# Linear attention with ReLU features: loads of two octets at a time, and one uniform loop in place of a loop with a hand-written end

## The chip, the cores and the metric

The kernel runs on one core of a Trainium2 chip. The metric is the device time of one execution in microseconds (us), as the median of several runs; lower is better. Durations of single instructions come from one profiled execution of the same kernel.

## The reference

```python
# Q, K, V: (8, 12, 512, 64) float32, 96 heads of 512 rows
Q_feat = np.maximum(0, Q)
K_feat = np.maximum(0, K)
KV = np.einsum('bhkd,bhkv->bhdv', K_feat, V)          # 64 x 64 per head
K_sum = np.sum(K_feat, axis=2)
numerator = np.einsum('bhqd,bhdv->bhqv', Q_feat, KV)
denominator = np.einsum('bhqd,bhd->bhq', Q_feat, K_sum)
out = numerator / (denominator[:, :, :, None] + 1e-10)
```

## The kernel before

The 96 heads are worked in 12 octets of eight heads (`NO` = 12), and an octet's K and V in two groups of four heads (`NG` = 24; octet `o` has the groups `2o` and `2o+1`). An octet's K, V and Q are 1 MB each in float32. All loads but those of octet 0's K and V go through POOL's DMA queue and are cast to bf16 on the way, so that a profile that counts the bytes written shows half of them. An octet's result is stored as 1 MB of float32.

The work of one octet `o`, by its functions:

- `prep(g)`: VectorE (DVE) makes the ReLU of K of group `g`, masked in two ways (`kf`, two instructions), and the first masked copy of V (`vo`, one). `prep_v(g, eng)` makes the second masked copy of V, on ScalarE (ACT) or on DVE. Both copies are needed by the matmuls of that group.
- `mm_kv(g)`: 16 matmuls on TensorE (PE) that sum K^T V of a group into its half of the PSUM tile `ps_kv`.
- `evac_kv(o, gs, share)`: four copies from `ps_kv` to the block-diagonal weights `kvd`, on ACT (with `share`, two of the four on DVE).
- `transp`, `relu_q`, `qt(o)`: 16 PE transposes of an octet's Q in two halves, and the ReLU of each half on ACT, which gives `qt`.
- `denom(o)`: 16 small matmuls for the denominators, then on DVE a masked add (`own`), a reduction (`den`) and a reciprocal (`rec`).
- `out_t(o)`: eight matmuls in two halves of four, each half copied from PSUM to `ot_sb` by ACT.
- `back(o, j)`: eight PE transposes (float32) of half `j` of `ot_sb` into PSUM; `norm(o, j, ...)`: DVE multiplies that half by `rec` into `o_sb`. `backs(o)` does both halves and then calls `store(o)`.
- `idle(n, o)`: `n` matmuls whose result nobody reads, in the last octets.

Instructions of one engine run in the order in which the program writes them; engines wait for one another through semaphores. PSUM has two buffers for the outputs of `out_t` and `back` together (`pou`), and two for the transposes of Q (`pqt`).

In SBUF there is a ring of `RING` = 6 octets for K, V and Q. At the start the loads of octets 1 to 6 are queued, two octets a transfer (`FIRST`): K, V, Q of octets 1 and 2, then of 3 and 4, then of 5 and 6. Each `store(o)` for `o` from 1 to 5 is followed on POOL's queue by the loads of octet `o + 6`: in three transfers for octets 7 and 8, in five (K and V by groups) for octets 9 to 11 (`PAIRS` = 9). The last two octets are stored from SP's queue, octet 11 in two halves.

For octets 0 to 8 (`SAME` = 8) one iteration of the loop is: `mm_kv` of both groups, `evac_kv(o)`, `prep` and `prep_v` (on ACT) of the next octet's first group, `backs(o - 1)`, `denom(o)`, `out_t(o)`, `prep` and `prep_v` (on DVE) of the next octet's second group, `qt(o + 1)`. From octet 8 on the order changes: `mm_kv` and `evac_kv` of the next octet stand ahead of `qt(o + 1)`, and `backs(o)` follows in the same iteration. The last two octets are written out one step after another, with `evac_kv` by groups and part of ACT's work given to DVE.

Of the kernel before, what the change touches and what calls it, by code (L numbers as in the profile page):

```python
# [10 lines left out]
def kernel(  # L11
# [7 lines left out]
    nc = tc.nc  # L19
    B, H, S, D = Q.shape  # L20
    assert D == 64
    P = 128
    D1 = D + 1
# [4 lines left out]
    RQ = S * 8 // P  # L28
    NHG = 4
    U = RQ // 2  # L30
    NG = NH // NHG
    NO = NG // 2
# [3 lines left out]
    fp32 = mybir.dt.float32  # L36
    bf16 = mybir.dt.bfloat16
    Act = mybir.ActivationFunctionType
# [50 lines left out]

    q_sb, k_sb, v_sb = {}, {}, {}  # L90

    PAIRS = NO - 3
    RING = DELAY + 1
    FIRST = (2, 2, 2)
    k_all = consts.tile([P, 2 * RING, R, D], bf16, name="k_all")
    v_all = consts.tile([P, 2 * RING, R, D], bf16, name="v_all")
    q_all = consts.tile([P, RING + 1, U, 2 * D], bf16, name="q_all")
# [6 lines left out]

    def load_kv(X, tile_, first, n):
        to = 2 * ((first // 2 - 1) % RING) + first % 2
        if n == 1:
            nc.gpsimd.dma_start(out=tile_[:, to].rearrange("p r d -> p (r d)"), in_=X[first], single_packet=True)  # L108
            return
        nc.gpsimd.dma_start(out=tile_[:, to:to + n].rearrange("p n r d -> p n (r d)"),  # L110
                            in_=X[first:first + n].rearrange("n p f -> p n f"), single_packet=True)

# [13 lines left out]
    load_q(0)  # L126
    make_identity(nc, ident)

    def load_octet(o, n=1):
        m = 1 if o >= PAIRS else 2 * n  # L130
        for g in range(2 * o, 2 * (o + n), m):
            load_kv(Kr, k_all, g, m)
            load_kv(Vr, v_all, g, m)
        load_q(o, n)

    o = 1
    for n in FIRST:
        load_octet(o, n)
        o += n
    assert o == RING + 1  # L140

    def zero_masks():
        for h in range(NHG):
# [48 lines left out]
    def prep(g):  # L192
        kf[g] = kfp.tile([P, R, 2, D], bf16, name="kf")
        for s in range(2):
            nc.vector.tensor_scalar(kf[g][:, :, s, :], k_sb[g], scalar1=0.0,  # L195
                                    scalar2=mask[:, 0, s:s + 1], op0=Alu.max, op1=Alu.mult)
        nc.vector.tensor_scalar(vo[g % NB][:, :, 0, 2:D + 2], v_sb[g], scalar1=mask[:, 1, 0:1],  # L197
                                scalar2=None, op0=Alu.mult)

    def prep_v(g, eng):  # L200
        if eng is nc.scalar:
            nc.scalar.activation(vo[g % NB][:, :, 1, 2:D + 2], v_sb[g], Act.Copy, scale=mask[:, 1, 1:2])  # L202
        else:
            nc.vector.tensor_scalar(vo[g % NB][:, :, 1, 2:D + 2], v_sb[g], scalar1=mask[:, 1, 1:2],  # L204
                                    scalar2=None, op0=Alu.mult)

    def mm_kv(g):
        for r in range(R):
            nc.tensor.matmul(  # L209
                ps_kv[:, g % 2, 0:2 * (D + 2)].rearrange("p (t d) -> p t d", t=2),  # L210
                kf[g][:, r, :, :].rearrange("p s d -> p (s d)"), vo[g % NB][:, r, :, 1:D4 - 1],
                start=(r == 0), stop=(r == R - 1), skip_group_check=True)


    def evac_kv(o, gs, share=False):
        for s in range(2):
            for c in range(2):
                copy = nc.vector.tensor_copy if share and c == 1 else nc.scalar.copy
                copy(  # L219
                    kvd[o % NK][64 * c:64 * c + 64, 4 * gs.start + s:4 * gs.stop:2,  # L220
                               c * D1:c * D1 + D1].rearrange(
                        "p (g t) d -> p g t d", t=2),
                    ps_kv[64 * s:64 * s + 64, gs, 0:2 * (D + 2)].rearrange(
                        "p g (t d) -> p g t d", t=2)[:, :, :, c:c + D1])


    def transp(o, i):
        ps = pqt.tile([P, U // 2, P], bf16, name="ps_qt")
        for u in range(U // 2):
            nc.tensor.transpose(ps[:, u, :], q_sb[o][:, i * (U // 2) + u, :], ident)  # L230
        return ps

    def relu_q(o, i, ps, eng=None):
        to = qt_sb[o % NZ][:, i * (U // 2):(i + 1) * (U // 2)]
        if eng is nc.vector:
            nc.vector.tensor_scalar(to, ps, scalar1=0.0, scalar2=None, op0=Alu.max)
        else:
            nc.scalar.activation(to, ps, Act.Relu)  # L238

    def qt(o):  # L240
        for i in range(2):
            relu_q(o, i, transp(o, i))


    def idle(n, o):
        for i in range(n):
# [2 lines left out]

    def out_t(o, halves=range(2)):
        if halves[0] == 0:
            ot[o] = otp.tile([P, U, 8, 16], fp32, name="ot_sb")
        q = qt_sb[o % NZ].rearrange("p u (h c) -> p u h c", h=8)
        for j in halves:
            ps = pou.tile([P, 4, U, 16], fp32, name="ps_ot", tag="ps_out")
            for i in range(4):
                h = 4 * j + i
                nc.tensor.matmul(ps[:, i], kvd[o % NK][:, h, 1:2 * D + 1], q[:, :, h, :],  # L260
                                 start=True, stop=True, skip_group_check=True)
            nc.scalar.copy(ot[o][:, :, 4 * j:4 * j + 4], ps.rearrange("p h u c -> p u h c"))  # L262
# [3 lines left out]
    def denom(o):  # L266
        ps = ps_den[:, 0].rearrange("p (u h c) -> p u h c", u=U, h=8)
        for u in range(U):
            nc.tensor.matmul(ps[:, u], qt_sb[o % NZ][:, u, :], kvd[o % NK][:, :, 0:2 * D1:2 * D1 - 1],  # L269
                             start=True, stop=True, skip_group_check=True)  # L270
        own = rcp.tile([P, U, 8, 2], fp32, name="own")
        nc.vector.scalar_tensor_tensor(
            own.rearrange("p u h c -> p u (h c)"), ps.rearrange("p u h c -> p u (h c)"), 1e-10,
            mask_h.rearrange("p h c -> p (h c)").unsqueeze(1).to_broadcast([P, U, 16]),
            op0=Alu.add, op1=Alu.mult)
        den = rcp.tile([P, RQ], fp32, name="den")
        nc.vector.tensor_reduce(out=den.rearrange("p (u c) -> p u c", c=2),  # L277
                                in_=own.rearrange("p u h c -> p u c h"), op=Alu.add,
                                axis=mybir.AxisListType.X)
        rec[o] = rcp.tile([P, RQ], fp32, name="rec")  # L280
        nc.vector.reciprocal(rec[o], den)
# [9 lines left out]
    def norm(o, j, ps, o_sb):  # L291
        rs = slice(16 * j, 16 * j + 16)
        nc.vector.tensor_tensor(o_sb[:, rs], ps,  # L293
                                rec[o][:, rs].unsqueeze(2).to_broadcast([P, 16, D]), op=Alu.mult)
# [3 lines left out]

    def store(o, o_sb):
        Ov = Or[o].rearrange("p (r d) -> p r d", d=D)  # L300
        if o == NO - 1:
            for j in range(2):
                rs = slice(RQ // 2 * j, RQ // 2 * (j + 1))
                nc.sync.dma_start(out=Ov[:, rs], in_=o_sb[:, rs])
            return
        if o >= NO - 2:
            nc.sync.dma_start(out=Ov, in_=o_sb)
            return
        nc.gpsimd.dma_start(out=Ov, in_=o_sb, single_packet=True)  # L309
        if 0 < o < NO - RING:  # L310
            load_octet(o + RING)

    def out_tile():
        return outp.tile([P, RQ, D], fp32, name="o_sb", tag="o_sb")

    both = slice(0, 2)
    zero8()
    nc.vector.tensor_copy(ident32, ident)
    nc.vector.tensor_reduce(out=mask8k, in_=ident32.rearrange("p (t s b) -> p s t b", t=4, s=2),
# [12 lines left out]
    def backs(o):  # L332
        o_sb = out_tile()
        for j in range(2):
            norm(o, j, back(o, j), o_sb)
        store(o, o_sb)

    def kvs(o):
        mm_kv(2 * o)
        mm_kv(2 * o + 1)  # L340
        evac_kv(o, both)

    SAME = NO - 4
    for o in range(NO - 2):
        if 0 < o <= SAME:
            kvs(o)
        prep(2 * o + 2)
        prep_v(2 * o + 2, nc.scalar)  # L350
        if 0 < o <= SAME:
            backs(o - 1)
        denom(o)
        out_t(o)
        prep(2 * o + 3)
        prep_v(2 * o + 3, nc.vector)
        if o >= SAME:
            kvs(o + 1)
        qt(o + 1)
        if o >= SAME:  # L360
            backs(o)

    o = NO - 2
    g = 2 * NO - 2
    prep(g)
    prep_v(g, nc.vector)
    denom(o)
    out_t(o)
    mm_kv(g)
    evac_kv(o + 1, slice(0, 1))  # L370
    prep(g + 1)
    prep_v(g + 1, nc.vector)

    o_sb = out_tile()
    norm(o, 0, back(o, 0), o_sb)
    ps = back(o, 1)
    mm_kv(g + 1)
    evac_kv(o + 1, slice(1, 2), share=True)
    for i in range(2):
        relu_q(o + 1, i, transp(o + 1, i), nc.vector if i == 1 else None)  # L380
    norm(o, 1, ps, o_sb)
    store(o, o_sb)
    idle(5, o + 1)
    out_t(o + 1, (0,))
    denom(o + 1)
    out_t(o + 1, (1,))
    idle(6, o + 1)
    backs(o + 1)
# [1 line left out]
_INS = ['Q', 'K', 'V']  # L390
_OUTS = [((8, 12, 512, 64), 'float32')]
# [25 lines left out]
```

## Time and profile before

| | |
|---|---|
| median of 3 runs | 126.01 us (125.93 to 126.33) |
| the profiled execution | 126.86 us, of which the span from the first to the last instruction is 125.1 us |
| busy, share of the span | PE 86.3 us (69%), DVE 83.2 us (67%), ACT 80.6 us (64%), POOL 26.5 us (21%) |
| mean granted PE clock | 0.931 |
| HBM | 37.75 MB read, 12.58 MB written: 402 GB/s over the span |

How to read the views: the page cuts the span into 40 equal slices, and a digit is the busy share of a slice in tenths (9 is 90% or more); `PEclk` is the granted PE clock in the same way, `DMA` the mean busy share of the 16 DMA engines. The chain that ended last is followed back from the last instruction, at each step to what released it; in order of time its lines read: start, duration, what. A timeline row reads: start, duration, engine, line, operation, tiles, shapes, number of instructions merged, and in brackets the idle time of the engine before it and who ended it. A row of windows gives a stretch's busy time and number of instructions on each engine, the granted PE clock, the share of DMA and GB/s. `L209` is line 209 of the kernel; busy matmuls are pipelined and their ends are modelled.

### The profile page before, as it was taken

The numbers are of one execution on the slowest core, as the hardware profiler recorded it, in microseconds if no ns is written. First come the engines' busy times: TensorE is split into PE (matmuls) and PEld (weight loads), VectorE is DVE, ScalarE is ACT, GpSimd is POOL, SyncE is SP. The second block draws the span as 40 slices with busy tenths as digits, with TensorE's granted clock in tenths as the row PEclk, the third lists the DMA queues.
The fourth block names the chain that finished last, engine by engine and source line by source line (L and its number), as shares of the span: only waits on it lengthen the run. The fifth ranks groups of instructions, "written<-read, shape, count | busy, mean of one in ns | idle before, by whom it ended". The sixth has DMA issues, their size and how long they took to land.

```text
span 125.1 us, 2615 instructions
## 1 busy us (share of the span) xinstructions
PE 86.3 (69%) x1067; PEld 77.6 (62%) x1067; DVE 83.2 (67%) x192; ACT 80.6 (64%) x112; POOL 26.5 (21%) x47
## 2 busy tenths in 40 slices
PE   0005884089898998959989897799596496888500
PEld 0005563089787897839978786698494494876400
DVE  2719716920997979797297984967909819977700
ACT  0009966544989989896598988658669466646000
POOL 6942020000100901203311122144333321000000
PEclk9999999558999999995999999859999999999995
DMA  4999999999999999999999999999999999999991
GB/s 84 389 321 206 212 210 217 214 210 210 215 219 208 212 212 218 214 321 419 217 204 307 282 218 264 324 212 238 347 214 226 356 224 216 349 422 424 430 390 76
DMA packets 9836, 32.67 MB, mean 261 GB/s; under 512 B 736, under 2 KB 736, under 8 KB 8160
## 3 DMA queue, kind: packets, MB, share of 16 engines
q0 software_dynamic: 9104, 28.31, 94.5%
q1 hardware_dynamic: 576, 3.15, 6.6%
q10 hardware_dynamic: 144, 1.05, 2.2%
q8 instruction: 8, 0.13, 0.4%
q14 instruction: 4, 0.03, 0.1%
HBM read 37.75 MB, written 12.58 MB: 402 GB/s over the span
## 4 chain that ended last, share of the span: by engine, by line
DMA 44%; DVE 23%; PE 19%; POOL 4%; ACT 2%; issue 2%; DVEq 1%; POOLq 0%
DMA q_all<-in_Q_dram 28%; DMA v_all<-in_V_dram 16%; DVE o_sb L293 13%; PE ps_kv L209 8%; PE ps_bk L287 6%; PE ps_qt L230 3%; DVE kf L195 3%; ACT ot_sb L262 2%; DVE vo_all L197 2%; PE ps_ot L260 1%; DVE vo_all L204 1%; POOL k_all L110 1%; POOL v_all L110 1%; DVE den L277 1%; DVEq L412 1%
## 5 line engine op out<-in xcount | busy, mean ns | idle before, releaser
L293 DVE TENSOR_TENSOR o_sb<-ps_bk,rec 128x1024 f32<-128x1024 f32 x24 | 28.3, 1218 | 20.0 <-PE ps_bk L287 20.0
L209 PE MATMUL ps_kv<-vo_all,kf 128*128 128x132 bf16 x352 | 26.9, 238 | 4.9 <-DVE vo_all L204 4.4
L209 PEld LDWEIGHTS <-kf 128*128 128x128 bf16 x352 | 24.8, 106 | 6.2 <-issue 3.5
L230 PE MATMUL ps_qt<-ident,q_all 128*128 128x128 bf16 x192 | 15.5, 245 | 15.9 <-DMA q_all<-in_Q_dram 15.8
L262 ACT COPY ot_sb<-ps_ot 128x1024 f32<-128x1024 f32 x24 | 24.0, 1013 | 3.8 <-PE ps_ot L260 2.9
L219 ACT CAST kvd<-ps_kv 64x260 bf16<-64x260 f32 (+1 forms) x46 | 16.5, 359 | 15.1 <-PE ps_kv L209 13.9
L238 ACT ACTIVATE qt<-ps_qt 128x1024 bf16<-128x1024 bf16 x23 | 22.4, 1025 | 3.6 <-PE ps_qt L230 3.5
L230 PEld LDWEIGHTS <-q_all 128*128 128x128 bf16 x192 | 13.7, 111 | 16.9 <-DMA q_all<-in_Q_dram 16.7
L287 PE MATMUL ps_bk<-ident,ot_sb 128*128 128x128 f32 x192 | 23.0, 273 | 0.4 <-ACT ot_sb L262 0.4
L287 PEld LDWEIGHTS ps_bk<-ident,ot_sb 128*128 128x128 f32 x192 | 20.8, 142 | 0.7 <-ACT ot_sb L262 0.7
L195 DVE TENSOR_SCALAR kf<-k_all,mask 128x1024 bf16<-128x1024 bf16 x44 | 18.3, 458 | 1.4 <-DMA k_all<-in_K_dram 1.3
L260 PE MATMUL ps_ot<-qt,kvd 128*128 128x256 bf16 x96 | 13.9, 272 | 6.2 <-DVE o_sb L293 5.5
L260 PEld LDWEIGHTS <-kvd 128*128 128x128 bf16 x96 | 8.9, 97 | 8.8 <-issue 7.0
L309 POOL DMA_DIRECT2D out_dram<-o_sb x10 | 5.5, 551 | 39.8 <-DVE o_sb L293 31.0
L202 ACT ACTIVATE vo_all<-v_all,mask 128x1024 bf16<-128x1024 bf16 x10 | 11.5, 1154 | 1.3 <-DMA v_all<-in_V_dram 1.2
L197 DVE TENSOR_SCALAR vo_all<-v_all,mask 128x1024 bf16<-128x1024 bf16 x22 | 10.6, 483 | 2.1 <-DMA v_all<-in_V_dram 2.1
L269 PEld LDWEIGHTS <-qt 128*128 128x128 bf16 x192 | 6.7, 96 | 4.9 <-ACT qt L238 2.0
L269 PE MATMUL ps_den<-kvd,qt 128*128 128x16 bf16 x192 | 7.3, 179 | 3.0 <-ACT kvd L189 1.7
L178 ACT ACT_TABLE_LOAD x1 | 1.3, 1283 | 9.7 <-DMA v_first<-in_V_dram 9.7
L204 DVE TENSOR_SCALAR vo_all<-v_all,mask 128x1024 bf16<-128x1024 bf16 x12 | 5.8, 480 | 0.0
L110 POOL DMA_DIRECT2D v_all<-in_V_dram x5 | 4.0, 810 | 7.8 <-ACT ot_sb L262 4.4
L108 POOL DMA_DIRECT2D k_all<-in_K_dram x6 | 3.6, 604 | 8.4 <-DMA q_all<-in_Q_dram 4.9
(36 smaller groups left out, 56.7 us busy)
## 6 DMA issues: line engine op xcount, KB each, us to landing
out_dram<-o_sb POOLq DMA_DIRECT2D x10, 1024.0 KB, 15.2
q_all<-in_Q_dram POOLq DMA_DIRECT2D x6, 512.0 KB, 13.8
k_all<-in_K_dram POOLq DMA_DIRECT2D x3, 1024.0 KB, 26.9
v_all<-in_V_dram POOLq DMA_DIRECT2D x3, 1024.0 KB, 31.0
q_all<-in_Q_dram POOLq DMA_DIRECT2D x3, 1024.0 KB, 35.1
k_all<-in_K_dram POOLq DMA_DIRECT2D x6, 256.0 KB, 13.4
v_all<-in_V_dram POOLq DMA_DIRECT2D x6, 256.0 KB, 12.3
v_first<-in_V_dram ACTq DMA_DIRECT2D x1, 1024.0 KB, 8.9
```

The source lines that it names most:

```text
L195: nc.vector.tensor_scalar(kf[g][:, :, s, :], k_sb[g], scalar1=0.0, scalar2=mask[:, 0, s:s + 1], op0=Alu.max, op1=Alu.mult)
L197: nc.vector.tensor_scalar(vo[g % NB][:, :, 0, 2:D + 2], v_sb[g], scalar1=mask[:, 1, 0:1], scalar2=None, op0=Alu.mult)
L202: nc.scalar.activation(vo[g % NB][:, :, 1, 2:D + 2], v_sb[g], Act.Copy, scale=mask[:, 1, 1:2])
L209: nc.tensor.matmul(ps_kv[:, g % 2, 0:2 * (D + 2)].rearrange("p (t d) -> p t d", t=2), kf[g][:, r, :, :].rearrange("p s d -> p (s d)"), vo[ ...
L219: copy(kvd[o % NK][64 * c:64 * c + 64, 4 * gs.start + s:4 * gs.stop:2, c * D1:c * D1 + D1].rearrange("p (g t) d -> p g t d", t=2), ps_kv[6 ...
L230: nc.tensor.transpose(ps[:, u, :], q_sb[o][:, i * (U // 2) + u, :], ident)
L238: nc.scalar.activation(to, ps, Act.Relu)
L260: nc.tensor.matmul(ps[:, i], kvd[o % NK][:, h, 1:2 * D + 1], q[:, :, h, :], start=True, stop=True, skip_group_check=True)
L262: nc.scalar.copy(ot[o][:, :, 4 * j:4 * j + 4], ps.rearrange("p h u c -> p u h c"))
L269: nc.tensor.matmul(ps[:, u], qt_sb[o % NZ][:, u, :], kvd[o % NK][:, :, 0:2 * D1:2 * D1 - 1], start=True, stop=True, skip_group_check=True)
L287: nc.tensor.transpose(ps[:, 2 * v:2 * v + 2].rearrange("p c d -> p (c d)"), ot[o][:, 8 * j + v].rearrange("p h c -> p (h c)"), ident32)
L293: nc.vector.tensor_tensor(o_sb[:, rs], ps, rec[o][:, rs].unsqueeze(2).to_broadcast([P, 16, D]), op=Alu.mult)
```

## The change

Loads: the list `RUNS` gives the octets of every transfer, (2, 2, 2, 2, 2, 1). The first three runs are queued at the start as before. The later ones hang on the store that frees their ring places: octets 7 and 8 together follow `store(1)`, octets 9 and 10 follow `store(3)`, octet 11 follows `store(4)`; K, V and Q are one transfer each. There are 18 transfers for octets 1 to 11 in place of 30.

Order of work: one loop for all octets. In it `mm_kv` of the first group stands first, then the former octet's `back` and `norm`, then `mm_kv` of the second group, then `evac_kv` of the whole octet on ACT, then the former octet's store. `prep_v` on ACT of the next octet's first group moves from ahead of `denom` and `out_t` to behind them. The separate order of the last four octets, the evacuation by groups and the sharing with DVE are gone, and octet 11 is stored as one transfer. The dummy matmuls stay, five behind the last `evac_kv` and six ahead of the last `backs`.

```diff
-    PAIRS = NO - 3
     RING = DELAY + 1
-    FIRST = (2, 2, 2)
+    RUNS = (2, 2, 2, 2, 2, 1)
...
-    def load_octet(o, n=1):
-        m = 1 if o >= PAIRS else 2 * n
-        for g in range(2 * o, 2 * (o + n), m):
-            load_kv(Kr, k_all, g, m)
-            load_kv(Vr, v_all, g, m)
+    def load_octets(o, n):
+        load_kv(Kr, k_all, 2 * o, 2 * n)
+        load_kv(Vr, v_all, 2 * o, 2 * n)
         load_q(o, n)
 
-    o = 1
-    for n in FIRST:
-        load_octet(o, n)
+    o, later = 1, {}
+    for n in RUNS:
+        if o <= RING:
+            load_octets(o, n)
+        else:
+            later[o + n - 2 - RING] = (o, n)
         o += n
...
     def store(o, o_sb):
...
-        if o == NO - 1:
-            for j in range(2):
-                rs = slice(RQ // 2 * j, RQ // 2 * (j + 1))
-                nc.sync.dma_start(out=Ov[:, rs], in_=o_sb[:, rs])
-            return
         if o >= NO - 2:
             nc.sync.dma_start(out=Ov, in_=o_sb)
             return
         nc.gpsimd.dma_start(out=Ov, in_=o_sb, single_packet=True)
-        if 0 < o < NO - RING:
-            load_octet(o + RING)
+        if o in later:
+            load_octets(*later[o])
...
             norm(o, j, back(o, j), o_sb)
-        store(o, o_sb)
+        return o_sb
...
-    SAME = NO - 4
-    for o in range(NO - 2):
-        if 0 < o <= SAME:
-            kvs(o)                       # mm_kv(2o), mm_kv(2o+1), evac_kv(o)
-        prep(2 * o + 2)
-        prep_v(2 * o + 2, nc.scalar)
-        if 0 < o <= SAME:
-            backs(o - 1)
+    for o in range(NO):
+        if o > 0:
+            mm_kv(2 * o)
+            o_sb = backs(o - 1)
+            mm_kv(2 * o + 1)
+            evac_kv(o)
+            store(o - 1, o_sb)
+        if o + 1 < NO:
+            prep(2 * o + 2)
+        else:
+            idle(5, o)
         denom(o)
         out_t(o)
-        prep(2 * o + 3)
-        prep_v(2 * o + 3, nc.vector)
-        if o >= SAME:
-            kvs(o + 1)
-        qt(o + 1)
-        if o >= SAME:
-            backs(o)
...                                       # the last two octets, lines 363 to 388
+        if o + 1 < NO:
+            prep_v(2 * o + 2, nc.scalar)
+            prep(2 * o + 3)
+            prep_v(2 * o + 3, nc.vector)
+            qt(o + 1)
+    idle(6, NO - 1)
+    store(NO - 1, backs(NO - 1))
```

More of the change, by code (lines that the diff above doesn't have):

```diff
@@ L106, in load_kv @@
         to = 2 * ((first // 2 - 1) % RING) + first % 2
-        if n == 1:
-            nc.gpsimd.dma_start(out=tile_[:, to].rearrange("p r d -> p (r d)"), in_=X[first], single_packet=True)
-            return
         nc.gpsimd.dma_start(out=tile_[:, to:to + n].rearrange("p n r d -> p n (r d)"),
@@ L127 @@
     make_identity(nc, ident)
-    def load_octet(o, n=1):
-        m = 1 if o >= PAIRS else 2 * n
-        for g in range(2 * o, 2 * (o + n), m):
-            load_kv(Kr, k_all, g, m)
-            load_kv(Vr, v_all, g, m)
-        load_q(o, n)
-    o = 1
-    for n in FIRST:
-        load_octet(o, n)
+    def load_octets(o, n):
+        load_kv(Kr, k_all, 2 * o, 2 * n)
+        load_kv(Vr, v_all, 2 * o, 2 * n)
+        load_q(o, n)
+    o, later = 1, {}
[4 more added lines that the diff above has]
+            later[o + n - 2 - RING] = (o, n)
         o += n
-    assert o == RING + 1
+    assert o == NO
     def zero_masks():
@@ L212, in mm_kv, with evac_kv @@
                 start=(r == 0), stop=(r == R - 1), skip_group_check=True)
-    def evac_kv(o, gs, share=False):
+    def evac_kv(o):
         for s in range(2):
             for c in range(2):
[L218 to L221, printed above, removed]
+                nc.scalar.copy(
+                    kvd[o % NK][64 * c:64 * c + 64, s::2, c * D1:c * D1 + D1].rearrange(
                         "p (g t) d -> p g t d", t=2),
-                    ps_kv[64 * s:64 * s + 64, gs, 0:2 * (D + 2)].rearrange(
+                    ps_kv[64 * s:64 * s + 64, :, 0:2 * (D + 2)].rearrange(
                         "p g (t d) -> p g t d", t=2)[:, :, :, c:c + D1])
@@ L231, in transp @@
         return ps
[L233 to L238, printed above, removed]
     def qt(o):
         for i in range(2):
-            relu_q(o, i, transp(o, i))
+            nc.scalar.activation(qt_sb[o % NZ][:, i * (U // 2):(i + 1) * (U // 2)], transp(o, i), Act.Relu)
     def idle(n, o):
@@ L248, in idle, with out_t @@
                              skip_group_check=True)
-    def out_t(o, halves=range(2)):
-        if halves[0] == 0:
-            ot[o] = otp.tile([P, U, 8, 16], fp32, name="ot_sb")
+    def out_t(o):
+        ot[o] = otp.tile([P, U, 8, 16], fp32, name="ot_sb")
         q = qt_sb[o % NZ].rearrange("p u (h c) -> p u h c", h=8)
-        for j in halves:
+        for j in range(2):
             ps = pou.tile([P, 4, U, 16], fp32, name="ps_ot", tag="ps_out")
@@ L300, in store @@
         Ov = Or[o].rearrange("p (r d) -> p r d", d=D)
-        if o == NO - 1:
-            for j in range(2):
-                rs = slice(RQ // 2 * j, RQ // 2 * (j + 1))
-                nc.sync.dma_start(out=Ov[:, rs], in_=o_sb[:, rs])
-            return
         if o >= NO - 2:
@@ L309, in store @@
         nc.gpsimd.dma_start(out=Ov, in_=o_sb, single_packet=True)
-        if 0 < o < NO - RING:
-            load_octet(o + RING)
+        if o in later:
+            load_octets(*later[o])
     def out_tile():
         return outp.tile([P, RQ, D], fp32, name="o_sb", tag="o_sb")
-    both = slice(0, 2)
     zero8()
@@ L335, in backs @@
             norm(o, j, back(o, j), o_sb)
-        store(o, o_sb)
[L338 to L341, printed above, removed]
-    SAME = NO - 4
-    for o in range(NO - 2):
-        if 0 < o <= SAME:
-            kvs(o)
-        prep(2 * o + 2)
-        prep_v(2 * o + 2, nc.scalar)
-        if 0 < o <= SAME:
-            backs(o - 1)
+        return o_sb
[10 more added lines that the diff above has]
+            idle(5, o)
         denom(o)
         out_t(o)
-        prep(2 * o + 3)
-        prep_v(2 * o + 3, nc.vector)
-        if o >= SAME:
-            kvs(o + 1)
-        qt(o + 1)
-        if o >= SAME:
-            backs(o)
[L363 to L388, printed above, removed]
+        if o + 1 < NO:
[5 more added lines that the diff above has]
+    store(NO - 1, backs(NO - 1))
 _INS = ['Q', 'K', 'V']
```

## The prediction

> **What bounds the kernel now.** I read the page first: which resource is full, and where.
>
> ```profile
> PE 86.3 (69%) x1067; PEld 77.6 (62%) x1067; DVE 83.2 (67%) x192; ACT 80.6 (64%) x112; POOL 26.5 (21%) x47
> ...
> PEclk9999999558999999995999999859999999999995
> DMA  4999999999999999999999999999999999999991
> ```
>
> No engine reaches 70%, while the 16 DMA engines are full from the second slice to the next to last. The transfers land in the order of their issue, so the end is the last landing. The chain that ended last agrees: its longest pieces are landings (the octet pair 3 and 4's Q until 41.3, octet 8's V until 76.8).
>
> ```profile
> 6.16 35.12 DMA q_all<-in_Q_dram
> ...
> 56.70 20.10 DMA v_all<-in_V_dram
> ...
> 106.72 1.11 PE ps_kv L209 x16
> 107.82 1.75 PE ps_bk L287 x16
> 109.57 0.96 PE ps_kv L209 x16
> 110.53 0.02 issue
> 110.56 0.27 ACT kvd L219
> ```
>
> The last five lines matter for another reason: for its last octet the old kernel already runs the order that the change puts everywhere (group, former octet's transposes, group, evacuation). From the first matmul to the evacuation it takes 110.56 - 106.72 = 3.84 us.
>
> So compute has slack now. How much, the timelines of ACT and PE show where data were at hand:
>
> ```profile
> 60.86 1.57 ACT L219 CAST kvd<-ps_kv 64x260 bf16<-64x260 f32 x4 [1.81 <-PE ps_kv L209]
> 62.45 1.15 ACT L202 ACTIVATE vo_all<-v_all,mask 128x1024 bf16<-128x1024 bf16 x1
> 63.65 2.09 ACT L262 COPY ot_sb<-ps_ot 128x1024 f32<-128x1024 f32 x2
> 65.63 1.95 ACT L238 ACTIVATE qt<-ps_qt 128x1024 bf16<-128x1024 bf16 x2
> 67.95 1.57 ACT L219 CAST kvd<-ps_kv 64x260 bf16<-64x260 f32 x4 [0.38 <-PE ps_kv L209]
> ...
> 62.48 0.58 PE L269 MATMUL ps_den<-kvd,qt 128*128 128x16 bf16 x16
> 62.95 0.60 PE L260 MATMUL ps_ot<-qt,kvd 128*128 128x256 bf16 x4
> ```
>
> From evacuation to evacuation is 67.95 - 60.86 = 7.1 us, and ACT is nearly never idle in it. The queue needs about 10 us an octet: one store (2.5 us a landing) and three loads; the loads of octets 5 and 6 land from 41.3 to 56.2, 7.45 us an octet. With 7.1 against 10, stores wait in the queue and the transfers never stop.
>
> **The change part by part.**
>
> *The loop.* I follow ACT, whose order becomes evacuation, copies of `out_t`, `prep_v` of the next first group, ReLU of Q. That `prep_v` writes the operand of the next `mm_kv`, the first matmul of the next iteration. PE then does group, both `back` halves, group, and only then can ACT evacuate. This closes a circle through ACT and PE, in which nothing runs beside anything else:
> - evacuation 1.57 us; 0.05 until `denom` starts (first octet: evacuation ends at 19.77, `denom` starts at 19.82);
> - `denom` until the first half of `out_t` starts, 0.48 (46.11 to 46.59); that half 0.61; 0.03 to ACT;
> - two copies 1.93 (the row at 96.30, where both halves were ready), then `prep_v` 1.15, less 0.1 in which ACT's rows overlap;
> - 0.05 to PE, then the 3.84 above.
>
> Sum: 1.57 + 0.05 + 0.48 + 0.61 + 0.03 + 1.93 + 1.15 - 0.1 + 0.05 + 3.84 = 9.6 us an octet, for 7.1 now. In the old order `prep_v` ran while PE was busy, and the `back` transposes ran while ACT evacuated; both covers are gone. Beside the circle: ReLU 1.95 on ACT during the 3.84; Q's transposes (1.06) during the copies; DVE's 6.4 us an octet, with the norms after the first `back` half and the second group's `prep` long before its matmuls. The `norm` rows no longer stand between the halves of `out_t` (0.54 idle there now); that gain is off the circle.
>
> *The start.* Before octet 1's evacuation, at 30.25 now, the 16 `back` transposes come in between (107.66 to 109.41, 1.75): 32.0. Ten circles later the last evacuation starts at 32.0 + 96 = 128.0.
>
> *The tail.* Evacuation, `denom`, `out_t` and copies: 1.57 + 0.05 + 0.48 + 0.61 + 0.03 + 1.93 = 4.67. From the end of the copies to the end of the last `norm`, 3.54 (115.35 to 118.89 now). So the last store is issued at 136.2. The dummy matmuls lie under the evacuation (five) and the copies (six, 0.82): nothing on the path. The whole store on an empty queue has no row. The halves took 5.2 each behind other stores, octet 10's whole one 8.1 behind two; from below, a landing spacing of 2.5 plus the 1 us between the first loads' issue at 0.74 and the DMA engines' first work. I take 5.2, the nearest, and keep 3.5 and 8.1. From landing to the end 0.9 (124.16 to 125.07). Span: 136.2 + 5.2 + 0.9 = 142.3.
>
> *The clock.* Matmuls at half clock: 32 of `mm_kv` took 3.14 at 81.46 against 2.18 at 42.22, so 0.48 a group. What brings that state:
>
> ```profile
> 53.08:56.49 3.41, 2.08 (x31) 1.45 (x29) 3.34 (x7) 3.25 (x4) 0.00 (x0) 1.00 1.04 326
> 76.97:80.39 3.42, 1.63 (x25) 1.29 (x22) 3.36 (x5) 2.21 (x3) 1.06 (x2) 1.00 1.02 347
> 80.39:83.80 3.41, 3.41 (x36) 3.41 (x33) 2.63 (x7) 2.73 (x3) 1.06 (x2) 0.50 1.12 218
> 87.21:90.62 3.41, 1.75 (x23) 1.44 (x22) 3.27 (x8) 2.26 (x3) 1.31 (x2) 1.00 1.02 345
> ```
>
> The first two stretches of 3.4 us were followed by half clock (for the first, from 56.5 to 59.9), the last was not, though PE was busy for 1.75 in it, less than the first one's 2.08. What the first two have in common is what they hold: `denom`, `out_t` and a few transposes, no `mm_kv`, and of `back` at most the end. In the new circle the 3.4 us after an evacuation's start hold just that. The clock changed at points 3.41 us apart, so perhaps one octet in three lines up: 3 x 0.48 = 1.5, an estimate, between 0 and 10. Rule of the Trainium skill, "TensorE: Matmul & The Clock Gate", section "Why this matters for your kernels": only a gap of over about 3 us between bursts brings the half clock back. The longest gap in the stretch at 76.97 was 1.25 us, so the trace speaks against it; by the rule the loop, whose longest gap is 1.7, would pay nothing and the sum be 1.5 less.
>
> *The transfers.* Fewer issues, 0.5 to 0.9 us each on POOL, which was 21% busy: nothing. Same bytes; octets 5 and 6 in three transfers of 1024 KB take 14.9 us, octet 10 in five from 91.7 to 99.1, 7.4. No gain in size. With such spacings the new order lands octets 7 and 8 at 76.2, 9 and 10 at 96.2, 11 at 106.2. The loop transposes the next octet's Q some 3.1 us after an evacuation starts: Q of octets 3, 5, 7, 9 and 11 at 44.7, 63.9, 83.1, 102.3 and 121.5, landed at 41.3, 56.2, 76.2, 96.2 and 106.2. So after octet 2 nothing waits for a load. A store on POOL's queue holds up the loads behind it: `store(3)`, normalised near 61.3, stands ahead of 9 and 10, `store(4)` near 71 ahead of 11; the queue then still holds 7 and 8, so that costs nothing. POOL lets eight transfers be outstanding (its ninth, at 10.97, waited for the first to land); no place frees too late. After `store(8)`, near 116, the DMA engines run empty; compute sets the end.
>
> *Sum.* 142.3 + 1.5 = 143.8 of span. The profiled execution is 126.86 for a span of 125.1, 1.8 more, and the median is 0.85 below it: 143.8 + 1.8 - 0.85 = 144.8 us, from 141 (shortest store, circle 9.4) to 150 (circle 9.8, longest store).
>
> **Rivals.**
> - *The half clock in every octet.* For it: any octet may meet the pattern. Per octet one group, 0.48, and up to as much again in `out_t` or the second group: about 1.0 x 10 on 143.3, so 153. Against it: stretches move against a 9.6 us loop. 0.12.
> - *Late pairs, not the circle, set the end.* If an overlap that I don't see shortens the circle below 8.6, Q of 9 and 10, landing at 96.2, holds up octet 9: its evacuation comes at 96.2 + 1.0 + 3.84 = 101, two more periods of 7.1, then 4.67 + 3.54 + 5.2 + 0.9 and 0.95 outside: 130.5. Against it: each link of the circle is a data dependency in the code. 0.09.
> - *Faster: larger transfers move more per us.* If the 1024 KB loads ran 10% faster, 9 and 10 would land 4 us earlier; with a loop at 7.1 that gives 126.5, and more speed down to about 124, where the stores of the last octets fill the queue. It decides from about 10% on, and only if the circle also fails. Against it: the 14.9 and 7.4 above. 0.05. The Trainium skill, "DMA: Bandwidth & Descriptors", section "Rules for kernel authors", asks for 1 MiB and more a transfer; by it the split loads would be the slow ones, which this trace does not show.
>
> **How the numbers follow.** Forecast 0.74, rivals 0.12, 0.09, 0.05. The predicted time is 144.8. The range reaches from 138 (a circle of 9.1 and the shortest store: 144.8 - 5 - 1.7) to 153, the half-clock case, and leaves out the last two rivals and the worst of the second. About 0.3% (0.4 us) is what a measurement of this kernel can tell from no change. Faster needs the third rival at its end: 0.03; same 0.02; slower 0.95.
>
> **What would show it.** Right: ACT's evacuations 9.4 to 9.9 us apart from octet 1 to 11, each waiting for PE's `ps_kv`; `ps_kv` of the first groups waiting for ACT's `vo_all` (a wait that does not exist now); no waits of PE for `q_all` after 26 us; DMA digits that fall from about the 33rd slice; the last evacuation near 128, three half-clock stretches. Wrong: DMA digits at 9 to the end, or evacuations 7 to 8.5 us apart, would mean that the circle is not closed; PEclk at 5 every octet, the first rival; a last store well off 5.2 us moves the end by as much.

## The result, and the profile after

The changed kernel takes 148.19 us, the median of four runs (146.79 to 149.52), against 125.97 for the kernel before (four runs): slower by a ratio of 1.168 (95% interval 1.162 to 1.175). It was forecast at 144.8, with a range of 138 to 153. The ratio is taken from the three of five executions whose mean PE clock was 0.881 to 0.884 (146.79, 147.05 and 147.98 us), while the traced one, 149.52 us with a span of 147.5, had 0.860. By the ratio, the loss is 16.8% of the time before, about 21 us.

Page of the changed kernel: busy shares, granted PE clock and DMA in 40 slices of 3.7 us.

```profile
PE 94.8 (64%) x1067; PEld 86.5 (59%) x1067; DVE 82.4 (56%) x188; ACT 80.1 (54%) x112; POOL 20.6 (14%) x35
...
PEclk9999997579995995987975899959869757999995
DMA  4999999999999999999999999999993600601506
```

The work of DVE and ACT is the same as before to within 1 us, but its share of the span has fallen. The DMA engines are full from the second slice to the thirtieth, until about 111 us, and then mostly empty: they no longer set the end. The PE clock, which fell in three places before, now falls in eight.

ACT's timeline over one octet at full clock, and PE's over the same octet:

```profile
83.90 1.57 ACT L217 CAST kvd<-ps_kv 64x260 bf16<-64x260 f32 x4 [4.07 <-PE ps_kv L208]
86.63 1.93 ACT L250 COPY ot_sb<-ps_ot 128x1024 f32<-128x1024 f32 x2 [1.17 <-PE ps_ot L248]
88.44 1.17 ACT L201 ACTIVATE vo_all<-v_all,mask 128x1024 bf16<-128x1024 bf16 x1
89.50 1.93 ACT L232 ACTIVATE qt<-ps_qt 128x1024 bf16<-128x1024 bf16 x2
93.56 1.57 ACT L217 CAST kvd<-ps_kv 64x260 bf16<-64x260 f32 x4 [2.13 <-PE ps_kv L208]
```

```profile
85.52 0.58 PE L257 MATMUL ps_den<-kvd,qt 128*128 128x16 bf16 x16 [1.71 <-ACT kvd L217]
85.94 1.03 PE L248 MATMUL ps_ot<-qt,kvd 128*128 128x256 bf16 x8
86.81 1.06 PE L227 MATMUL ps_qt<-ident,q_all 128*128 128x128 bf16 x16
89.66 1.11 PE L208 MATMUL ps_kv<-vo_all,kf 128*128 128x132 bf16 x16 [1.79 <-ACT vo_all L201]
90.60 1.92 PE L275 MATMUL ps_bk<-ident,ot_sb 128*128 128x128 f32 x16
92.36 1.11 PE L208 MATMUL ps_kv<-vo_all,kf 128*128 128x132 bf16 x16
```

Read the brackets in turn and the circle is there: PE waits 1.71 us for the evacuation, ACT waits 1.17 for `out_t`, PE waits 1.79 for ACT's `vo_all`, ACT waits 2.13 for the second group. From evacuation to evacuation it is 93.56 - 83.90 = 9.66 us. The waits over the whole run show the new one by name: ten times, once an octet.

```profile
PE ps_den L257 <- ACT kvd L217: 18.2, 11, 1.7
ACT ot_sb L250 <- PE ps_ot L248: 14.8, 12, 1.6
...
PE ps_kv L208 <- ACT vo_all L201: 10.4, 10, 1.8
```

### The profile page after: what moved, and what is told of

The parts are those of the page before. It is cut to its first block, busy times and chain, and to the rows that moved or that the text cites. A ratio compares the mean times of both kernels' runs of the same rounds, so it can differ in the third digit from the quotient of the medians.

```text
span 147.5 us, 2597 instructions
## 1 busy us (share of the span) xinstructions
PE 94.8 (64%) x1067; PEld 86.5 (59%) x1067; DVE 82.4 (56%) x188; ACT 80.1 (54%) x112; POOL 20.6 (14%) x35
## 4 chain that ended last, share of the span: by engine, by line
PE 44%; ACT 28%; DMA 15%; issue 6%; POOL 1%; ACTq 1%; DVE 1%; DVEq 1%; POOLq 0%
PE ps_kv L208 17%; PE ps_bk L275 16%; DMA q_all<-in_Q_dram 15%; ACT kvd L217 11%; ACT ot_sb L250 9%; ACT vo_all L201 8%; PE ps_ot L248 5%; PE ps_den L257 4%; PE ps_qt L227 2%; DVE o_sb L281 1%; DVEq L363 1%; ACTq L363 1%; POOL v_all L106 0%; POOL k_all L106 0%; POOL ident masks.py:199 0%
## 5 line engine op out<-in xcount | busy, mean ns | idle before, releaser
L217 ACT CAST kvd<-ps_kv 64x260 bf16<-64x260 f32 x44 | 16.4, 374 | 30.3 <-PE ps_kv L208 29.5
L227 PE MATMUL ps_qt<-ident,q_all 128*128 128x128 bf16 x192 | 20.0, 287 | 14.5 <-DMA q_all<-in_Q_dram 14.5
L227 PEld LDWEIGHTS <-q_all 128*128 128x128 bf16 x192 | 18.3, 135 | 15.5 <-DMA q_all<-in_Q_dram 14.8
L275 PE MATMUL ps_bk<-ident,ot_sb 128*128 128x128 f32 x192 | 26.2, 296 | 1.0 <-ACT ot_sb L250 1.0
L275 PEld LDWEIGHTS ps_bk<-ident,ot_sb 128*128 128x128 f32 x192 | 24.2, 157 | 1.3 <-ACT ot_sb L250 1.3
L248 PE MATMUL ps_ot<-qt,kvd 128*128 128x256 bf16 x96 | 15.3, 313 | 0.0
L201 ACT ACTIVATE vo_all<-v_all,mask 128x1024 bf16<-128x1024 bf16 x11 | 12.8, 1164 | 0.0
L196 DVE TENSOR_SCALAR vo_all<-v_all,mask 128x1024 bf16<-128x1024 bf16 x22 | 10.6, 482 | 0.0
L260 DVE SCALAR_TENSOR_TENSOR own<-ps_den,mask_h 128x256 f32<-128x256 f32 x12 | 5.1, 424 | 7.9 <-PE ps_den L257 7.9
L184 PE MATMUL ps_kv<-vo_all,kf 128*128 128x264 bf16 x32 | 5.7, 356 | 0.6 <-ACT vo_all L177 0.6
```

What stands on the lines that cost most here:

```text
L217: nc.scalar.copy(kvd[o % NK][64 * c:64 * c + 64, s::2, c * D1:c * D1 + D1].rearrange("p (g t) d -> p g t d", t=2), ps_kv[64 * s:64 * s + 6 ...
L275: nc.tensor.transpose(ps[:, 2 * v:2 * v + 2].rearrange("p c d -> p (c d)"), ot[o][:, 8 * j + v].rearrange("p h c -> p (h c)"), ident32)
```

## The experiments

Times are medians; each ratio is against the kernel before, run on the same chip beside it, with its 95% interval. First, the two halves of the change apart.

### The loads alone, and the loop alone

The first kernel is the old loop with the new loads (the definitions of the loads are changed with it, as in the change itself):

```diff
...
-        if 0 < o < NO - RING:
-            load_octet(o + RING)
+        if o in later:
+            load_octets(*later[o])
```

> The kernel before with only the new loads (octets 7 and 8, 9 and 10 together behind store(1) and store(3), octet 11 behind store(4)). Theory that the circle through ACT and PE makes the whole loss: the loop stays at 7.1 us an octet, Q of octet 9 lands at 96.2 instead of 89.2 and holds octet 9 up; from there three octets at about 7.5 us and the old tail give 127 to 130 us. Theory that the pairs of octets make the loss: 140 us or more. If larger transfers moved more per us: 126 or less.

131.44 us, ratio 1.037 (1.031 to 1.044). PE's timeline shows what the pair does:

```profile
72.89 2.14 PE L261 MATMUL ps_ot<-qt,kvd 128*128 128x256 bf16 x8 [3.42 <-DVE o_sb L294]
76.10 1.89 PE L231 MATMUL ps_qt<-ident,q_all 128*128 128x128 bf16 x16 [1.06 <-DMA q_all<-in_Q_dram]
```

The Q of octets 7 and 8 lands at 76.1; before the change octet 7's landed at 69.4. The 3.42 us ahead of `out_t` is the same lateness by another way: DVE's `norm` stands behind a `prep` that waits for the pair's V. Octet 9 waits again, near 96. The evacuations of octets 6 and 7 are 13.3 us apart, the others from octet 1 on up to there 7.1 to 7.4. This cost a little more than the 127 to 130 us that were expected.

The second is the new loop with the old loads:

```diff
...
-        if o in later:
-            load_octets(*later[o])
+        if 0 < o < NO - RING:
+            load_octet(o + RING)
```

> The changed kernel with the old loads (one octet behind each store, octets 9 to 11 in five transfers). Theory of the circle: no change against the changed kernel, evacuations 9.6 us apart at full clock, 146 to 150 us, and no matmul waits for Q after 26 us. Theory of the pairs: back near 126 to 130 us.

147.45 us, ratio 1.166 (1.157 to 1.175), the same as the whole change. So the loop makes the loss, and the loads, which cost 4.8 us by themselves, add nothing to it: a loop that needs 9.66 us an octet reaches no octet before its load has landed.

### Opening the circle, link by link

One line moved, ACT's copy of V:

```diff
             prep(2 * o + 2)
+            prep_v(2 * o + 2, nc.scalar)
...
         out_t(o)
         if o + 1 < NO:
-            prep_v(2 * o + 2, nc.scalar)
```

> The changed kernel with one line moved: ACT's masked copy of V of the next first group stands ahead of denom and out_t again. Theory of the circle: the copy (1.15 us) and its way to PE leave the circle; PE goes on from Q's transposes to the next group; the period is evacuation 1.57, denom and out_t and transposes about 2.5, then 3.84: about 7.9 us. Then Q of octet 9, landing at 96.2, holds up octet 9, and the end comes near 131 to 133 us. Rival: ACT's work an octet (6.7 us) and the order of the groups alone make the loss; then a period above 9 stays, 143 us or more.

134.46 us, ratio 1.063 (1.060 to 1.066), for 1.168 with the whole change: some 13 of the 21 us lost were in the place of one ACT instruction an octet. ACT's timeline:

```profile
32.96 1.57 ACT L217 CAST kvd<-ps_kv 64x260 bf16<-64x260 f32 x4 [4.02 <-PE ps_kv L208]
34.55 1.15 ACT L201 ACTIVATE vo_all<-v_all,mask 128x1024 bf16<-128x1024 bf16 x1
35.73 1.93 ACT L250 COPY ot_sb<-ps_ot 128x1024 f32<-128x1024 f32 x2
37.54 1.96 ACT L232 ACTIVATE qt<-ps_qt 128x1024 bf16<-128x1024 bf16 x2
40.72 1.57 ACT L217 CAST kvd<-ps_kv 64x260 bf16<-64x260 f32 x4 [1.22 <-PE ps_kv L208]
```

The copy of V now runs where ACT had waited for `out_t`, and the period is 7.76 at full clock. In the four octets where the clock was halved it was 9.32 or 9.33, and octet 9, which also waits for its Q, took 10.45; that is why the time is above the expected 131 to 133.

The other link, the second group ahead of the evacuation:

```diff
             mm_kv(2 * o)
-            o_sb = backs(o - 1)
             mm_kv(2 * o + 1)
             evac_kv(o)
+            o_sb = backs(o - 1)
```

> The changed kernel with both groups' mm_kv ahead of the evacuation and the former octet's back and norm behind it; ACT's masked copy of V stays behind out_t. Theory of the circle: the 1.75 us of back lie under the evacuation, but out_t's second half waits for norm again; period about 8.1 us, octet 9 close to its load at 96.2, 132 to 135 us. Rival, that the masked copy of V alone closes the loop: no more than 1 us less than the changed kernel's 147.

133.73 us, ratio 1.058 (1.053 to 1.062), periods of 8.28 to 8.6 apart from octet 9's wait. Opening either link alone brings most of the loss back, as a circle asks. But both edits together (the two diffs above in one kernel):

> The changed kernel with both links opened: both groups ahead of the evacuation, and ACT's masked copy of V ahead of denom and out_t. The new loads, the uniform loop to the end and the whole last store stay. Theory of the circle: period 7.1 to 7.5 us as before the change, held up by Q of octet 9 at 96.2: 96.2 + 1.0 + 1.9 to the evacuation of octet 9 at 99, two periods of 7.5, then 4.7 + 3.5 + back 1.75 + a store of 3.9 + 0.9, and 1 outside the span: about 130 us. If the uniform end itself costs more than the late pair, above 134.

133.81 us, ratio 1.061 (1.055 to 1.067), and again 8.28 to 8.6. That was a miss: a period of 7.1 to 7.5 and about 130 us were expected. So something else held the period, the same in both kernels. PE and DVE in the kernel with both links opened:

```profile
81.45 1.11 PE L208 MATMUL ps_kv<-vo_all,kf 128*128 128x132 bf16 x16 [1.42 <-DVE vo_all L203]
82.39 1.92 PE L275 MATMUL ps_bk<-ident,ot_sb 128*128 128x128 f32 x16
...
89.74 1.11 PE L208 MATMUL ps_kv<-vo_all,kf 128*128 128x132 bf16 x16 [1.42 <-DVE vo_all L203]
```

```profile
83.47 2.36 DVE L281 TENSOR_TENSOR o_sb<-ps_bk,rec 128x1024 f32<-128x1024 f32 x2 [2.08 <-PE ps_bk L275]
85.75 0.87 DVE L194 TENSOR_SCALAR kf<-k_all,mask 128x1024 bf16<-128x1024 bf16 x2
...
89.20 0.48 DVE L203 TENSOR_SCALAR vo_all<-v_all,mask 128x1024 bf16<-128x1024 bf16 x1
91.76 1.22 DVE L281 TENSOR_TENSOR o_sb<-ps_bk,rec 128x1024 f32<-128x1024 f32 x1 [2.08 <-PE ps_bk L275]
```

DVE waits 2.08 us for `back`, then works `norm`, `prep`, `own`, `prep` without a gap, and its last instruction (at 89.20) is what PE's second group waits for (1.42, until 89.74); the next `back` stands behind that group. A second circle, DVE and PE, of 91.76 - 83.47 = 8.29 us. The old loop had `prep` of the next octet ahead of `norm`, where it fills DVE's wait. Putting that back too:

```diff
             mm_kv(2 * o)
             mm_kv(2 * o + 1)
             evac_kv(o)
-            o_sb = backs(o - 1)
-            store(o - 1, o_sb)
         if o + 1 < NO:
             prep(2 * o + 2)
             prep_v(2 * o + 2, nc.scalar)
-        else:
-            idle(5, o)
+        if o > 0:
+            store(o - 1, backs(o - 1))
```

> Both links opened and also the next octet's first prep on DVE ahead of the former octet's norm, as in the old loop; new loads, uniform loop to the end (the five dummy matmuls left out), whole last store. Theory that DVE closed a second circle in the two runs before (8.3 us: norm 2.4, prep 1.2, own/den/rec 1.15, prep and prep_v 1.65, then the second group 0.95 and the first back half 0.9): period 7.1 now, waits for the pairs' Q at 76 and 96, end 131 to 133 us. Theory that the period of 8.3 is PE's or ACT's: it stays at 8.3 and the time at 133.8.

130.48 us, a little under the expected 131 to 133, ratio 1.034 (1.032 to 1.037), periods of 7.1 to 7.35 and waits for the pairs: the second circle is shown. What remains over the kernel before is the late pair and the plain end, which the next run tells apart.

### The hand-written end, the last store, and the queue

The old order and the old loads, but one loop to the end, no evacuation by groups, a whole last store. It is the kernel with three links opened, with its loads put back:

```diff
...
-        if o in later:
-            load_octets(*later[o])
+        if 0 < o < NO - RING:
+            load_octet(o + RING)
```

> The old order inside the loop and the old loads, but no hand-written end: one loop for all octets, evacuation whole on ACT, last store whole. Compute waits for octet 11's Q (109.2); then transposes 1.1, two groups 1.9, evacuation 1.6, and 7.5 to the last norm give a last store near 121, 3.9 to land and 0.9: 126.5 to 128.5 us, 0 to 2 above before. If the end is worth more than that, 130 or more.

127.03 us, ratio 1.006 (1.003 to 1.010): the hand-written end is worth about 0.8 us, and the late pairs cost the other 3.5. Of that, the split of the last store alone, taken out of the kernel before:

```diff
-        if o == NO - 1:
-            for j in range(2):
-                rs = slice(RQ // 2 * j, RQ // 2 * (j + 1))
-                nc.sync.dma_start(out=Ov[:, rs], in_=o_sb[:, rs])
-            return
```

> The kernel before with the last octet stored in one transfer. It is issued at 118.9 instead of halves at 117.8 and 118.9. A whole store on an empty queue took 3.9 us in the changed kernel, the last half took 5.2 behind others: landing near 124, so no change within 0.5 us; at most 1.2 us more if the half megabyte that starts 1.1 us later comes last.

126.38 us, ratio 1.0006 (0.998 to 1.003): nothing that can be measured.

Loads of one octet, each one store earlier, in the kernel before:

```diff
-        if 0 < o < NO - RING:
-            load_octet(o + RING)
+        if o < NO - RING - 1:
+            load_octet(o + RING + 1)
```

> The kernel before with each later octet's loads one store earlier (octet 7 behind store(0), octet 11 behind store(4)), sizes as before. Last Q lands about 2.5 us earlier, near 106.8. Theory that the full DMA queue sets the old end: the stores fill the same queue, so 125.5 to 126.2 us. Theory that the last octet's work after its last load sets it (15.8 us from the landing of Q to the end): up to 1.5 us less, 124.5 us.

126.34 us, ratio 1.0008 (0.998 to 1.004). Yet compute did end sooner: SP's timeline has the last halves at 114.2 and 115.4, where the kernel before issued them at 117.8 and 118.9. The windows tell where it went:

```profile
110.00:115.00 5.00, 3.27 (x28) 2.63 (x26) 3.29 (x6) 1.73 (x2) 0.00 (x0) 1.00 1.01 426
115.00:120.00 5.00, 0.00 (x0) 0.00 (x0) 0.34 (x1) 0.00 (x0) 0.00 (x0) 0.60 1.00 423
120.00:122.00 2.00, 0.00 (x0) 0.00 (x0) 0.00 (x0) 0.00 (x0) 0.00 (x0) 0.50 0.90 371
```

No engine works from about 115.4 on, and the DMA engines are full (1.00, then 0.90) to 122. So with these loads the full queue sets the end, and 3.5 us of earlier compute were worth nothing; the kernel before, with its DMA engines as full to 121 us, stands at the same limit. No kernel here beats the one before.

### The half clock

Dummy matmuls in PE's two idle places of the changed kernel:

```diff
+    def fill(n, o):
+        for i in range(n):
+            j = i % (U // 2)
+            nc.tensor.matmul(ps_den[:, 1], ident, q_sb[o][:, 2 * j:2 * j + 2, :], start=True, stop=True,
+                             skip_group_check=True)
...
             prep(2 * o + 2)
+            if o > 0:
+                fill(10, o)
...
             qt(o + 1)
+            if o > 0:
+                fill(8, o + 1)
```

> The changed kernel with dummy matmuls (128x256) in PE's two idle places of octets 1 to 10: ten behind the evacuation's start and eight behind Q's transposes; nobody reads them, and they fit into the 1.7 us of each place. Theory that the half clock comes from stretches with little streamed through PE: no half clock after 31 us, every period 9.6, the last evacuation near 129 and the end near 143 us. Theory that only an idle gap of over 3 us brings it, or that it comes whatever PE does: unchanged, 146 to 150 us.

216.35 us: a mistake of mine in the edit. The dummies read Q's ring place behind `store(o - 1)`, which had queued the next load into that place, so each waited for a load that nobody else needed yet (PE waited 70.3 us in three such waits). With a constant tile as their operand:

```diff
-            nc.tensor.matmul(ps_den[:, 1], ident, q_sb[o][:, 2 * j:2 * j + 2, :], start=True, stop=True,
-                             skip_group_check=True)
+            nc.tensor.matmul(ps_den[:, 1], ident, filler, start=True, stop=True, skip_group_check=True)
...
+    filler = consts.tile([P, 2, P], bf16, name="filler")
+    for i in range(2):
+        nc.vector.tensor_copy(filler[:, i], ident)
```

> The dummy matmuls of the run before once more (ten behind each evacuation's start, eight behind Q's transposes, octets 1 to 10), but on a constant tile instead of Q, whose ring place the next load overwrites. Theory that the half clock comes from 3.4 us stretches with little streamed through PE: no half clock after 31 us, every period 9.6, last evacuation near 129, end near 143 us. Theory that only a gap of over 3 us brings it, or that it comes whatever PE does: 146 to 150 us as the changed kernel.

144.76 us, ratio 1.146 (1.142 to 1.150). Its page, and ACT's evacuations:

```profile
PEclk9999999569999999999999999999999999999997
```

```profile
81.09 1.57 ACT L217 CAST kvd<-ps_kv 64x260 bf16<-64x260 f32 x4 [2.12 <-PE ps_kv L208]
...
90.75 1.57 ACT L217 CAST kvd<-ps_kv 64x260 bf16<-64x260 f32 x4 [2.12 <-PE ps_kv L208]
```

From 31 us to the end of PE's work the clock is never halved, every period is 9.65 or 9.66 (the first 9.60), and the traced span is 142.3 us, 5.2 below the changed kernel's traced one. By the ratios, 1.168 and 1.146, the gain is about 2.8 us. The cost of the half clock varies: in the trace of the changed kernel two octets took 11.6 us, in that of the loop alone, with the same order of work and a span of 144.7, only one did. That is 2.0 of the 2.8 us between these two spans; the other 0.8 is there at the first evacuation already (32.98 against 32.15).

The dummies fill PE's idle time and shorten its gaps as well (0.6 and 0.9 us in place of 1.7 and 1.8), so this run alone does not tell which of the two counts. The traces do. The last number of a shape such as 128x132 is the number of columns that one matmul or transpose streams. The thirteen traces hold 162 stretches of 3.41 us at full clock without float32 transposes: all 49 that were followed by half clock streamed at most 3,004 columns, all 113 that were not at least 3,204. Neither the gap nor the busy time orders them so: the stretch from 53.08 of the kernel before, shown in the prediction, was followed by half clock with PE busy for 2.08 us and this as its longest gap:

```profile
56.21 1.66 PE L230 MATMUL ps_qt<-ident,q_all 128*128 128x128 bf16 x16 [0.79 <-DMA q_all<-in_Q_dram]
```

Here are one stretch of the changed kernel and one of the kernel with both groups ahead of the evacuation, each with the stretch behind it:

```profile
92.41:95.82 3.41, 1.70 (x36) 1.55 (x34) 2.84 (x6) 1.50 (x4) 0.61 (x1) 1.00 1.05 293
95.82:99.24 3.42, 3.18 (x24) 2.65 (x22) 2.67 (x7) 2.71 (x3) 0.00 (x0) 0.50 1.06 282
```

```profile
66.85:70.27 3.42, 1.63 (x22) 1.35 (x21) 3.35 (x9) 3.16 (x4) 0.61 (x1) 1.00 1.13 216
70.27:73.68 3.41, 3.41 (x45) 3.29 (x45) 1.33 (x4) 2.83 (x5) 0.70 (x1) 1.00 1.08 217
...
67.49 0.60 PE L248 MATMUL ps_ot<-qt,kvd 128*128 128x256 bf16 x4 [0.53 <-DVE o_sb L281]
67.92 1.06 PE L227 MATMUL ps_qt<-ident,q_all 128*128 128x128 bf16 x16
70.24 0.22 PE L208 MATMUL ps_kv<-vo_all,kf 128*128 128x132 bf16 x1 [1.26 <-ACT vo_all L201]
```

In the first, 15 matmuls of a group, the 16 small ones and three of `out_t` start: 15 x 132 + 16 x 16 + 3 x 256 = 3,004 columns, and the clock falls. In the second it is 4 x 256 + 16 x 128 + 132 = 3,204, and the clock stays, though PE is busy for less of it (1.63 against 1.70 us) and waits for 1.26 us in it.

## Why the prediction was right, step by step

- **The circle**: forecast 9.6 us, measured 9.65 to 9.66 at full clock. Opening either of its links gave some 13 and 14 us back. The loop alone has the whole loss, so the loads are no part of it. The circle is most of that loss, not all: the half clock is about 2.8 us of it and the plain end about 0.8, each measured in another kernel, so that they need not add up.
- **The start**: forecast 32.0 for the first evacuation, measured 32.98. The 16 `back` transposes came into a half-clock stretch (24.1 to 31.0) and took 2.56 us in the chain instead of 1.75, which is 0.8 of the 1.0. I had taken their full-clock duration from another place of the trace.
- **The half clock**: its direction was right, its size was the worst of the sum, 1.5 us forecast as three falls of 0.48. The ten periods add up to 134.49 - 32.98 = 101.5, which is 5.0 above ten of 9.65, and there were seven falls. Five lasted 3.4 us and cost 0.1 to 0.4 each. Most comes from two octets, where the clock was halved for 6.8 us and met this:

```profile
78.06 1.92 PE L208 MATMUL ps_kv<-vo_all,kf 128*128 128x132 bf16 x16 [1.06 <-ACT vo_all L201]
79.78 3.08 PE L275 MATMUL ps_bk<-ident,ot_sb 128*128 128x128 f32 x16
```

  The group took 0.8 longer and `back` 1.1 to 1.2, so 1.95 an octet. I had priced the group too low and left out `back`, which is on the circle as well: the row of 3.14 us from which the 0.48 came starts at 81.46, and the half clock ended at 83.80, so only part of it ran at half clock. The windows of the changed kernel show one fall: a stretch as I had described it, with no `mm_kv` but its last, then two at half clock.

```profile
71.93:75.34 3.41, 1.70 (x32) 1.49 (x30) 2.81 (x6) 1.80 (x5) 1.32 (x2) 1.00 1.06 263
75.34:78.76 3.42, 2.36 (x24) 2.19 (x22) 1.92 (x6) 3.42 (x4) 0.71 (x1) 0.50 1.00 417
78.76:82.17 3.41, 3.41 (x24) 3.41 (x22) 0.45 (x1) 1.07 (x2) 0.54 (x1) 0.50 1.09 260
```

  As a cause that description was only partly right. Two of the seven falls, the two long ones, followed such a stretch. The stretches ahead of the other five held 9 to 16 matmuls of `mm_kv`, as does the one at 92.41 above. What all seven have in common is that few columns were streamed (2,748 to 3,004).

  PE's longest gap in the loop was 1.8 us, so keeping the gaps under about 3 us, as the rule of the Trainium skill cited in the prediction asks, was not enough here. Another sentence of the Trainium skill bears on it, in "TensorE: Matmul & The Clock Gate", section "Part 4: PE-mode transpose": a transpose does not count as PE-busy in the same way for the clock gate. The traces of this case do not bear that out for the bf16 transposes of Q: the stretch at 66.85 above kept the clock with 16 of them and only 1,156 columns of other matmuls, while the one at 92.41 lost it with 3,004 columns and no transpose starting in it.
- **The tail**: forecast 4.67 + 3.54 = 8.2 from the last evacuation to the last `norm`; measured 134.49 to 142.69, 8.2.
- **The last store**: 5.2 taken, 3.9 measured on an empty queue, near the lower end of the bounds:

```profile
out_dram<-o_sb SPq DMA_DIRECT2D x2, 1024.0 KB, 3.9
```

- **The transfers**: Q of the pairs and of octet 11 forecast to land at 76.2, 96.2 and 106.2; they landed at 76.5, 96.8 and 106.6, and PE waited for none of them. The DMA engines ran empty near 112, earlier than the forecast 116, because `store(8)`, delayed with its octet, came at 114.0.
- **The sum**: against the forecast span of 143.8 the start added 1.0, the half clock 3.5, the circle's 0.05 in ten octets 0.5, and the store took 1.3 away: 147.5, the traced span. At full clock, with the dummy matmuls, the span was 142.3, exactly the forecast ahead of its clock term; that it is exact is luck, since the start and the circle are about 1.4 above their terms there and the store 1.3 below its own.
- **The rivals**: the late pair, priced at 130.5 with a loop of 7.1 us, is real once the circle is open: it takes 130.48 us with all three links opened, 131.44 with the old loop. That it comes so close is luck in part: the traced span with the links opened is 128.6, 1.0 below the priced one, and the time outside the span 1.0 above. Half clock in every octet did not come. Larger transfers moved no more per us: the landings above are those of the old spacing.

## What to carry to other kernels

When a program is limited by its queue of transfers, compute has slack that busy shares don't measure; before reordering, follow one iteration through every engine and ask whether the last instruction of one engine's turn is what the next engine's first one waits for. A circle of dependencies through in-order engines sets the period whatever the engines' loads are (here 9.66 us with no engine busy for more than about 7), and moving one instruction under another engine's work can open it. After opening one, look for the next: here a second circle of 8.3 us stood right behind the first.

## What the runs showed of the hardware that I had not expected

Float32 transposes slow with the PE clock too: 16 of them took 2.88 us in the chain at half clock and 1.75 at full clock. A loop with PE gaps of no more than 1.8 us lost the full clock seven times, and 18 dummy matmuls of 128x256 an octet kept it; what told the stretches apart was the columns streamed in 3.41 us, at most 3,004 where the clock fell and at least 3,204 where it stayed, bf16 transposes counted like matmuls and stretches with float32 transposes left out. A store of 1 MB on an empty queue lands 3.9 us after its issue, one of 512 KB in 2.6 to 2.8 (the two halves with the new loads in the old loop), so by estimate 1.4 us or so are not transfer at the 2.5 us a megabyte that the full queue shows.
